# Two-layer hybrid trunk, one core: modulation on VectorE as product and sum, VectorE work given out by TensorE time

## The chip, the cores and the metric

The kernel runs on one core of a Trainium2 chip, with no other core at work. The metric is the device time of one execution in microseconds (us); a profiled execution gives a trace beside it. Five engines work in parallel, each in its own order: TensorE (PE; its weight loads are PEld), VectorE (DVE), ScalarE (ACT), GpSimd (POOL) and SyncE (SP), which here only issues DMAs.

## The reference, cut to what matters

```python
c_act = jax.nn.silu(c)                                   # (1, 2048)
for l in range(2):
    mod = c_act @ w_ada[l] + b_ada[l]                    # (1, 6*2048): the modulation
    sh1, sc1, gt1, sh2, sc2, gt2 = jnp.split(mod, 6, -1)
    h = rms_norm(x, g_norm1[l]) * (1 + sc1) + sh1        # x: 256 tokens x 2048
    # w_in -> q, k, v, indexer, u, p;  A: sparse attention -> o_a;
    # C: trailing means of p -> o_c;  B: diagonal complex state space of u:
    #   states = scan over time of lam_bar * state + b_bar @ u   (32 groups x 64 states)
    #   y = gelu((c_t @ states).real + d_skip * u);  o_b = y * sigmoid(y @ w_glu)
    mix = (sum of sigmoid(h @ w_gate[i] + b) * (o_i @ p_i) over the branches) @ w_out[l]
    x = x + gt1 * mix
    h = rms_norm(x, g_norm2[l]) * (1 + sc2) + sh2
    x = x + gt2 * conv_ffn(h, w_up, conv_w, conv_b, w_down)   # d_ff 5504
```

All weights are f32 and each is read once, so all of them pass through the chip's memory during the run.

## The kernel before

**The stream.** All weights but the modulation's are cut into 936 slots of 128x1024 f32 (512 KB; some 128x656). For each slot SP issues the load of `raw`, ACT rounds it to `whi` (fp32r, TensorE's fast f32 form), DVE makes `wlo = raw - whi`, and PE multiplies both halves with the activations. In most slots these are 8 matmuls `b<-h,whi` of 512 columns (high and low half of the activations side by side) and 8 `b<-h,wlo` of 256. `run_stream` (from L383) walks the slots: `make_hi(s+3)`, `make_lo(s+2)`, the slot's matmuls, then `step()`. The stages of a layer, in slots: q, k, v, u, p and the gates with the branch projections, `w_glu` at 160, `p_b`, the rest of the gates, `w_out` from 178, `w_up` from 210, `w_down` in two parts from 302 and 426; layer 1 begins at 468.

**Side work.** Everything else is written as Python generators, which `step()` advances. Their instructions are put down at that point of the program, so the order on every engine is fixed when the kernel is built. DVE tasks run while `credit` is above zero: a slot adds 2.6 us, each DVE operation takes off a price by its size (`tt`, `stt`, `ts`, L153 to L168), and the credit is kept between -2 and 2. `require` (L215) forces a task to its end where a slot needs its result: `yh` (the state-space output) before `w_glu`, `oc` (the pooling branch) before `p_c`, `ob` before `p_b`, `mod` before the norms.

**Modulation (`ada_group`, L504).** `w_ada` comes as 384 tiles `adaw` of 512 KB, through a ring of 4 (8 for the first 64). `ADA` lists the groups of tiles, `ADA_PLAN` how far they may be by which slot. 192 tiles are done on PE, in steps of two tiles (8 records `b<-adaw,cact`, four at a time in the four column groups); the other 192 on DVE, two operations a tile into `acc` (128x512, `acc<-adaw,cact,acc`), and after every 8 tiles four PE transposes (L573) and a `TENSOR_REDUCE` (L549) that sum `acc` over the partitions. The task is stepped ahead of the others; a group on PE is forced, one step at a time while its `yield 1` comes back, and so back to back.

**State space (`s5_tables`, `s5_task`).** Four blocks of channels are taken one after the other, in two pairs of state columns each; `prod` holds the rotated inputs, two scans a column run over time on DVE (L1090), and a pair's sine and cosine tables `tb` for the 256 times are built by doubling: ACT writes `pr`, DVE adds 16, 32, 64 and 128 columns at a time, so that DVE waits for ACT at each of four stages. `yp` sums `b<-prod,cc` on PE; `yt`, `u`, `yh` are the end of the chain.

Of the kernel before, what the change touches and what calls it, by code (L numbers as in the profile page):

```python
# [38 lines left out]
NRAW, NHI, NLO, NADA, APRE = 4, 4, 3, 4, 4  # L39
# [41 lines left out]
ADA_PLAN = ((0, 18), (8, 34), (18, 50), (30, 66), (48, 66), (140, 128), (204, 160), (296, 192), (460, 296), (580, 320), (670, 356), (770, 384))  # L81


ADA = [(0, [(1, t), (0, t)], 2 if t < 4 else 4, True) for t in (0, 2, 4, 8, 12)]
for _l in range(DEPTH):
    if _l:
        ADA += [(_l, [(p, t + j) for j in (0, 4) for p in (1, 0)], 4, False) for t in (0, 8)]
    ADA += [(_l, [(2, t) for t in range(0, 16, 4)], 4, not _l)]
    ADA += [(_l, [(p, t + j) for j in (0, 4) for p in (4, 3)], 4, not _l or t == 0) for t in (0, 8)]
    ADA += [(_l, [(5, t) for t in range(0, 16, 4)], 4, False)]  # L90

# [29 lines left out]
class Kernel:  # L121
    def __init__(self, ctx, tc, a):
# [19 lines left out]
        self.x_save = dpool.tile([128, KT, T], F32, name="x_save")  # L142
        ctx.enter_context(tc.manual_schedule())
# [9 lines left out]
    def tt(self, out, a, b, op):  # L153
        self.credit -= 0.069 + 1.04e-3 * self.size(out)
        self.nc.vector.tensor_tensor(out, a, b, op=op)  # L155

    def stt(self, out, a, s, b, op0, op1):
        self.credit -= (0.069 if isinstance(s, float) else 0.13) + 1.04e-3 * self.size(out)
        self.nc.vector.scalar_tensor_tensor(out, a, s, b, op0=op0, op1=op1)  # L159

    def ts(self, out, a, s1, s2, op0, op1=None):
        self.credit -= 0.069 + 0.7e-3 * self.size(out)
# [5 lines left out]
    def vcopy(self, out, a):  # L168
        self.credit -= 0.069 + 0.7e-3 * self.size(out)
        self.nc.vector.tensor_copy(out, a)  # L170
# [8 lines left out]
    def mm(self, out, lhsT, rhs, start=True, stop=True):  # L179
        self.nc.tensor.matmul(out, lhsT, rhs, start=start, stop=stop)  # L180
# [17 lines left out]
    def step_task(self, t, force=False):  # L198

        while force or (self.credit > 0 and self.acredit > -1.0):  # L200
# [7 lines left out]
    def step(self):  # L208
        self.step_evacs()
        for t in list(self.low):  # L210
            self.step_task(t, force=self.ada_on_pe)
        for t in list(self.tasks):
            self.step_task(t)

    def require(self, *keys):  # L215

        for key in keys:
            n = 0
            while key not in self.done:
                self.step_evacs()  # L220
                for t in self.tasks + self.low:
                    if key[0] in t[1] or n > 20:
                        self.step_task(t, force=True)
# [90 lines left out]
    def block_emitter(self, bl):  # L314
        def emit(hi, lo):
# [13 lines left out]
            for i, high in enumerate((True, False) if self.high_first else (False, True)):  # L329
                for u, j, x, cnt in todo:  # L330
                    out, w, r = (u.ps, hi, x) if high else (u.ps[:, T:], lo, x[:, :T])

                    self.nc.tensor.matmul(out, w[:, j * 128:(j + 1) * 128], r, start=i == 0 and cnt == 1,  # L333
                                          stop=i == 1 and cnt == u.nk, skip_group_check=True)
# [6 lines left out]
    def block(self, u, k, hi, lo):  # L341
# [16 lines left out]
        for i, (w, r) in enumerate(ops):  # L358
            self.nc.tensor.matmul(ps, w, r, start=first and i == 0 and not u.after,  # L359
                                  stop=last and i == 2 and not u.before, skip_group_check=shared)  # L360
# [22 lines left out]
    def run_stream(self):  # L383
        n = len(self.slots)
        for s in range(n):
# [7 lines left out]
            self.credit = max(min(self.credit + 2.6 * o.w / SLOT, 2.0), -2.0)  # L393
            self.acredit = max(min(self.acredit + 2.6 * o.w / SLOT, 2.0), -2.0)
# [100 lines left out]
    def ada_fetch(self, upto):  # L495
        while self.ada_next < upto:
            i = self.ada_next
            pool, bufs = self.ada_ring if i < 64 and i % (NADA + APRE) < APRE else (self.cpool, NADA)
            t = pool.tile([128, 1024], F32, name="adaw", tag="adaw", bufs=bufs)
# [1215 lines left out]
```

## Time and profile before

| | |
|---|---|
| median of 3 runs | 2950.82 us (2948.54 to 2952.45) |
| profiled execution | 2947.58 us, span 2945.8 us |
| PE busy | 2863.4 us, 97% of the span |
| DVE busy | 2301.6 us, 78% |
| ACT busy | 1395.1 us, 47% |
| DMA | 705.97 MB, mean 240 GB/s |

The span runs from the first instruction to the last of the profiled execution. Idle time of PE is 2945.8 - 2863.4 = 82.4 us. [...]

### The profile page before, as it was taken

What the parts mean: (1) busy time and instruction counts of PE and PEld (TensorE: products, weight loads), DVE (VectorE), ACT (ScalarE), POOL (GpSimd) and SP (SyncE); (2) the same over time, 40 slices, a digit from 0 to 9 for tenths busy, and PEclk for the clock granted to TensorE, in tenths of its full rate; (3) what the DMA queues carried; (4) which work ended last, traced back from release to release, by engine and by line L of the source; (5) the groups of instructions that cost most, each with busy time, mean ns of one, the idle gap of its engine ahead of it and who ended that gap; (6) DMA issues with size and microseconds to landing.
All of it is one profiled execution on the core that took longest, in us unless ns stands there. A gap on an engine that the chain in (4) does not pass through costs nothing.

```text
span 2945.8 us, 45105 instructions
## 1 busy us (share of the span) xinstructions
PE 2863.4 (97%) x16880; PEld 2427.5 (82%) x16880; DVE 2301.6 (78%) x4222; ACT 1395.1 (47%) x2209; POOL 43.7 (1%) x74
## 2 busy tenths in 40 slices
PE   6999999979999999999999999999999999999998
PEld 3787787758788888888878788888888888888887
DVE  5888677766698899999966887899888877556664
ACT  3355544434455543455435455455445555345542
POOL 0000000000000000000000000000000000000000
PEclk9999999979999999999999999999999999999999
DMA  9867767747677778888886555576686776566664
GB/s 366 349 225 254 238 243 253 248 145 279 209 263 251 251 270 296 297 287 298 299 315 205 194 180 182 192 245 241 230 283 211 241 237 204 192 189 188 189 198 150
DMA packets 195387, 705.97 MB, mean 240 GB/s; under 512 B 22496, under 2 KB 23008, under 8 KB 195168
## 3 DMA queue, kind: packets, MB, share of 16 engines
q1 hardware_dynamic: 190656, 691.23, 68.7%
q0 software_dynamic: 3648, 11.01, 1.0%
q8 instruction: 132, 2.16, 0.3%
q10 hardware_dynamic: 864, 0.86, 0.1%
q14 instruction: 87, 0.71, 0.1%
HBM read 698.82 MB, written 4.19 MB: 239 GB/s over the span
## 4 chain that ended last, share of the span: by engine, by line
PE 87%; issue 6%; DVE 4%; DMA 1%; ACT 0%; POOL 0%; POOLq 0%; SPq 0%; DVEq 0%; ACTq 0%
PE b L333 69%; PE b L180 11%; PE b L359 6%; DVE wlo L155 1%; DMA adaw<-in_w_ada 1%; DVE acc L159 0%; PE b L573 0%; DVE prod L155 0%; DVE x L159 0%; POOL out L1501 0%; PE b L917 0%; DVE prod L1090 0%; DVE ftmp L164 0%; DVE ftmp L155 0%; PE b L821 0%
## 5 line engine op out<-in xcount | busy, mean ns | idle before, releaser
L155 DVE TENSOR_TENSOR wlo<-raw,whi 128x1024 fp32r<-128x1024 f32 x936 | 1132.7, 1213 | 485.6 <-issue 220.1
L175 ACT ACTIVATE whi<-raw 128x1024 fp32r<-128x1024 f32 x936 | 984.1, 1053 | 1028.2 <-PE b L333 630.0
L333 PE MATMUL b<-h,whi 128*128 128x512 f32 x4352 | 1058.4, 393 | 4.3 <-DVE h L159 4.3
L333 PEld LDWEIGHTS b<-h,whi 128*128 128x128 f32 x4352 | 798.6, 189 | 168.9 <-issue 12.2
L333 PEld LDWEIGHTS b<-h,wlo 128*128 128x128 f32 x4352 | 562.5, 191 | 42.2 <-issue 11.3
L333 PE MATMUL b<-h,wlo 128*128 128x256 f32 x4352 | 578.5, 284 | 0.0
L333 PE MATMUL b<-hid,whi 128*128 128x512 f32 x1376 | 330.4, 391 | 2.6 <-DVE hid L159 2.6
L333 PEld LDWEIGHTS b<-hid,whi 128*128 128x128 f32 x1376 | 252.6, 188 | 52.1 <-DVE hid L159 3.4
L159 DVE SCALAR_TENSOR_TENSOR acc<-adaw,cact,acc 128x512 f32<-128x512 f32 x360 | 269.0, 747 | 5.6 <-DMA adaw<-in_w_ada 0.5
L333 PEld LDWEIGHTS b<-hid,wlo 128*128 128x128 f32 x1376 | 176.7, 191 | 9.5 <-DVE wlo L155 1.9
L333 PE MATMUL b<-hid,wlo 128*128 128x256 f32 x1376 | 180.0, 283 | 1.3 <-DVE wlo L155 1.3
L180 PE MATMUL b<-whi,h 128*128 128x512 f32 (+1 forms) x512 | 155.3, 376 | 0.0
L175 ACT ACTIVATE fth<-ft 128x256 f32<-128x256 f32 x86 | 36.0, 418 | 196.2 <-DVE ft L159 196.2
L333 PE MATMUL b<-mh,whi 128*128 128x512 f32 x512 | 123.6, 392 | 4.7 <-DVE mh L155 4.7
L180 PE MATMUL b<-adaw,cact 128*32 128x512 f32 (+1 forms) x832 | 111.2, 584 | 7.7 <-DMA adaw<-in_w_ada 7.7
L180 PEld LDWEIGHTS b<-whi,h 128*128 128x128 f32 x512 | 94.1, 188 | 27.9 <-issue 9.5
L333 PEld LDWEIGHTS b<-mh,whi 128*128 128x128 f32 x512 | 93.9, 188 | 23.9 <-DVE mh L155 3.7
L180 PE MATMUL b<-wlo,h 128*128 128x512 f32 (+1 forms) x256 | 94.9, 371 | 0.0
L359 PE MATMUL b<-h,whi 128*128 128x256 f32 x384 | 77.1, 297 | 10.4 <-ACT whi L175 5.4
L159 DVE SCALAR_TENSOR_TENSOR ft<-fa,lvecs,ft 128x255 f32<-128x255 f32 (+1 forms) x172 | 82.5, 481 | 3.1
L359 PEld LDWEIGHTS b<-h,whi 128*128 128x128 f32 x384 | 64.5, 202 | 15.6 <-ACT whi L175 6.5
L159 DVE SCALAR_TENSOR_TENSOR tb<-tb,nsn,pr 128x16 f32<-128x16 f32 (+3 forms) x128 | 35.4, 276 | 47.9 <-ACT pr L175 47.5
(262 smaller groups left out, 2539.0 us busy)
## 6 DMA issues: line engine op xcount, KB each, us to landing
adaw<-in_w_ada SPq DMA_DIRECT2D x384, 512.0 KB, 5.4
raw<-in_w_up SPq DMA_DIRECT2D x344, 512.0 KB, 3.9
raw<-in_w_gate SPq DMA_DIRECT2D x192, 512.0 KB, 3.9
raw<-in_w_down_a SPq DMA_DIRECT2D x88, 512.0 KB, 4.0
raw<-in_w_down_b SPq DMA_DIRECT2D x84, 512.0 KB, 4.4
raw<-in_w_out SPq DMA_DIRECT2D x64, 512.0 KB, 4.9
raw<-in_w_q SPq DMA_DIRECT2D x32, 512.0 KB, 3.9
raw<-in_p_a SPq DMA_DIRECT2D x32, 512.0 KB, 4.4
```

The source lines that it names most:

```text
L155: self.nc.vector.tensor_tensor(out, a, b, op=op)
L159: self.nc.vector.scalar_tensor_tensor(out, a, s, b, op0=op0, op1=op1)
L175: self.nc.scalar.activation(out, a, func, bias=bias, scale=scale)
L180: self.nc.tensor.matmul(out, lhsT, rhs, start=start, stop=stop)
L333: self.nc.tensor.matmul(out, w[:, j * 128:(j + 1) * 128], r, start=i == 0 and cnt == 1, stop=i == 1 and cnt == u.nk, skip_group_check=True)
L359: self.nc.tensor.matmul(ps, w, r, start=first and i == 0 and not u.after, stop=last and i == 2 and not u.before, skip_group_check=shared)
```

## The change

- **Modulation on DVE** becomes one `tensor_tensor_reduce` a tile: `adaw` (now laid out with output channels on partitions and 1024 inputs along the row) times `crow`, a row of the activated c replicated on all partitions, summed into one column of `mod`. On the engine each is two instructions, 128x1024 and a 128x1. No transposes and no `acc` are left there. `crow` is made at the start by 16 PE matmuls, 4 ACT copies and a 1 MB DMA to memory (`c_rows`), and loaded back half by half (512 KB, 8 times in all) by POOL's queue.
- **Credit** is earned by each PE instruction, by its columns (`earn`), not by slot; the prices of DVE operations rise by about 0.085 us each (the scan's from 0.68 to 1.35).
- **Order**: DVE's modulation is stepped after the other tasks, not before them; a PE step yields `None`, so one step (two tiles) comes per slot; `ADA` and `ADA_PLAN` are rearranged; the ring of 4 becomes a ring of 3 and a fourth tile shared with `crow` that serves until tile 160. `require` advances a forced task one yield at a time.
- **Tables**: the angles of 16 low and 16 high digits (`e0`, `e1`) are built once a layer; the tables of a pair are six DVE operations of 512 (products, sum and difference), without ACT.
- **`w_out`** begins with its first four output tiles interleaved by k, and the reload of x moves from its second to its sixth slot.

```diff
-NRAW, NHI, NLO, NADA, APRE = 4, 4, 3, 4, 4
+NRAW, NHI, NLO, NADA, APRE = 4, 4, 3, 3, 4
+ADA_FIRST, ADA_PE = 64, 160
     def tt(self, out, a, b, op):
-        self.credit -= 0.069 + 1.04e-3 * self.size(out)
+        self.credit -= 0.155 + 1.04e-3 * self.size(out)
...
+    def mm(self, out, lhsT, rhs, start=True, stop=True, share=1, **kw):
+        n = self.size(rhs)
+        self.earn((n + 32) / 2400 if rhs.dtype == F32R else n / 600 / share)
+        self.nc.tensor.matmul(out, lhsT, rhs, start=start, stop=stop, **kw)
...
     def step(self):
         self.step_evacs()
-        for t in list(self.low):
-            self.step_task(t, force=self.ada_on_pe)
+        low = list(self.low)
+        for t in low:
+            if self.ada_on_pe:
+                self.step_task(t, force=True)
         for t in list(self.tasks):
             self.step_task(t)
+        for t in low:
+            if t in self.low and not self.ada_on_pe:
+                self.step_task(t)
...
-            self.credit = max(min(self.credit + 2.6 * o.w / SLOT, 2.0), -2.0)
+            self.credit = max(min(self.credit, 2.0), -2.0)
...
-                yield 1
+            yield 1 if i < ADA_FIRST else None
...
+    def ada_sums(self, i0, l, tiles, first, ahead, last):
+        i = i0
+        for h in (first, 1 - first):
+            self.ada_on_pe = False
+            if self.crow_half != h:
+                self.crow = self.cpool.tile([128, 1024], F32, name="crow", tag="crow", bufs=1)
+                self.nc.gpsimd.dma_start(self.crow, self.c_rows[:, h * 1024:(h + 1) * 1024])
...
+            for part, t in tiles:
+                self.ada_fetch(min(i + ahead, last))
+                w = self.ada_tiles.pop(i)
...
+                self.credit -= 0.16 + 1.04e-3 * 1024
+                self.nc.vector.tensor_tensor_reduce(w, w, self.crow, 1.0, seed, OP.mult, OP.add, col)
...
+    def s5_tables(self, s):
+        tb = self.mx.tile([128, 2, 2, T], F32, name="tb", tag="tb")
+        pr = self.mx.tile([128, 2, T], F32, name="pr", tag="prod", bufs=2)
...
+            self.tt(out, hi[x[0]], lo[x[1]], OP.mult)
+            self.tt(p4, hi[y[0]], lo[y[1]], OP.mult)
+            yield 1
+            self.tt(out, out, p4, op)
...
-        self.slots[n + 1].pre = load_x
+        self.slots[n + 5].pre = load_x
...
-        o = [(n, k) for ks in (range(12), range(12, KT)) for n in range(4) for k in ks]
+        o = [(n, k) for k in range(KT) for n in range(4)]
```

Where instructions moved, first on DVE ahead of `w_glu` of layer 0. `prod` and `tb` are the state space, `yt` and `yh` its output that the next slot needs. Before, the last `wlo` ahead of `yh`, and the first rows behind it:

```order
L155 TENSOR_TENSOR wlo<-raw,whi 128x1024
L155 TENSOR_TENSOR prod<-prod 128x256 x2
L1090 SCALAR_TENSOR_TENSOR prod<-r,prod 128x256 x2
L159 SCALAR_TENSOR_TENSOR prod<-prod,tb 128x256
L155 TENSOR_TENSOR prod<-prod,tb 128x256
L155 TENSOR_TENSOR prod<-prod,tb 128x2x256
```

Between the last of these and `yh` stand 33 more rows: the 16 `tb` rows of a pair's tables, one of the gates, two chains with scans and the four rows of `yt` and `u`. After, from the last `wlo` ahead of `yh` to the next:

```order
L163 TENSOR_TENSOR wlo<-raw,whi 128x1024
L167 SCALAR_TENSOR_TENSOR prod<-prod,tb 128x256
L163 TENSOR_TENSOR prod<-prod,tb 128x256
L163 TENSOR_TENSOR prod<-prod,tb 128x2x256
L163 TENSOR_TENSOR th_5985<-th_5985,b_6092 128x256
L167 SCALAR_TENSOR_TENSOR yt<-u,lvecs,b_5659 128x256
L174 TENSOR_SCALAR yt<-yt 128x256
L163 TENSOR_TENSOR yt<-yt 128x256
L167 SCALAR_TENSOR_TENSOR u<-yt 128x256
L163 TENSOR_TENSOR yh<-u,yh 128x256 x4
L163 TENSOR_TENSOR wlo<-raw,whi 128x1024 x2
```

The tables of the last pair and two chains with scans went to earlier slots; the last three `prod` rows and the chain of `yt` are what is still behind that `wlo`.

Second, on PE, the end of the first layer's `w_down`, where five steps of modulation stood in a row before:

```order
L573 MATMUL b_15201<-const,acc 128x128 x4
L333 MATMUL b_15156<-hid,whi 128x512 x6
L333 MATMUL b_15212<-hid,whi 128x512 x2
L333 MATMUL b_15156<-hid,wlo 128x256 x6
L333 MATMUL b_15212<-hid,wlo 128x256 x2
L180 MATMUL b_15232<-adaw,cact 32x512 x20
L333 MATMUL b_15212<-hid,wlo 128x256 x8
L333 MATMUL b_15212<-hid,whi 128x512 x16
```

Those 20 are gone from the end of `w_down`; that part of the modulation is on DVE now. The group that PE does in layer 1 now stands around the beginning of `p_c` (`oc` matmuls), one step in a slot, in seven slots that follow one another; its first steps:

```order
L191 MATMUL b_17452<-adaw,cact 32x512 x4
L191 MATMUL b_17469<-h,whi 128x512 x8
L191 MATMUL b_17469<-h,wlo 128x256 x8
L191 MATMUL b_17452<-adaw,cact 32x512 x4
L191 MATMUL b_17498<-kT,qT 128x256 x2
L191 MATMUL b_17469<-h,wlo 128x256 x8
L191 MATMUL b_17469<-h,whi 128x512 x8
L191 MATMUL b_17452<-adaw,cact 32x512 x4
L191 MATMUL b_17544<-p,wp 128x256 x2
```

Each step stands alone behind a slot's 16 matmuls, with a ring of three tiles behind it. (The trace has two records for each of these matmuls: a step is x4 here and x8 there.)

Third, on DVE, the pooling branch ahead of `p_c` in layer 0. `lg` and `mxv` belong to the attention, `oa` to its output. Before:

```order
L155 TENSOR_TENSOR wlo<-raw,whi 128x1024 x2
L155 TENSOR_TENSOR th<-th,b_3795 128x256
L159 SCALAR_TENSOR_TENSOR oc<-b_3849,lvecs,oc 128x256 x2
L159 SCALAR_TENSOR_TENSOR oc<-b_3852,lvecs,oc 128x256 x2
L155 TENSOR_TENSOR wlo<-raw,whi 128x1024
```

There `oc` has a stretch of its own, behind one row of the gates. After:

```order
L163 TENSOR_TENSOR wlo<-raw,whi 128x1024
L163 TENSOR_TENSOR lg<-b_3956,isc 128x512
L962 TENSOR_REDUCE mxv<-lg 128x2
L172 TENSOR_SCALAR mxv<-mxv 128x2
L968 RECIPROCAL mxv<-mxv 128x2
L172 TENSOR_SCALAR lg<-lg,mxv 128x256 x2
L163 TENSOR_TENSOR th<-th,b_3908 128x256
L167 SCALAR_TENSOR_TENSOR oc<-b_3974,lvecs,oc 128x256 x2
L167 SCALAR_TENSOR_TENSOR oc<-b_3984,lvecs,oc 128x256 x2
L163 TENSOR_TENSOR prod<-b_3901,tb 128x512 x2
L163 TENSOR_TENSOR prod<-prod 128x256 x2
```

`oc` now comes behind a piece of attention in the same stretch between two `wlo`.

## Rows read from the trace of the kernel before

**Rows 1.** The page's first part: busy us, share of the span, instructions.

```profile
PE 2863.4 (97%) x16880; PEld 2427.5 (82%) x16880; DVE 2301.6 (78%) x4222; ACT 1395.1 (47%) x2209; POOL 43.7 (1%) x74
```

**Rows 2.** Waits of PE: waited-for work, us in total, times, longest us.

```profile
PE b L180 <- DVE prod L155: 14.7, 4, 6.6
...
PE b L180 <- DMA adaw<-in_w_ada: 7.7, 12, 2.0
...
PE b L359 <- ACT yh L175: 5.1, 2, 2.6
PE b L333 <- DVE mh L155: 4.7, 2, 3.1
```

**Rows 3.** Windows: stretch, its us, busy us by engine, PE's clock, DMA share, GB/s.

```profile
606.00:634.00 28.00, 11.27 (x42) 4.39 (x42) 19.16 (x50) 6.95 (x19) 0.00 (x0) 0.55 0.10 35
213.00:606.00 393.00, 393.00 (x2397) 309.82 (x2396) 301.80 (x641) 191.36 (x358) 6.35 (x9) 1.00 0.71 243
1050.00:1500.00 450.00, 446.86 (x2581) 394.19 (x2581) 431.40 (x749) 208.03 (x278) 5.96 (x11) 1.00 0.84 295
...
54.00:64.00 10.00, 7.38 (x32) 1.00 (x28) 2.56 (x15) 0.60 (x3) 0.00 (x0) 1.00 1.03 417
...
633.60:639.20 5.60, 5.57 (x24) 5.33 (x24) 1.54 (x6) 0.90 (x3) 0.00 (x0) 0.50 0.01 3
```

**Rows 4.** Timeline of DVE ahead of `w_glu`, layer 0: start us, us, instructions, count.

```profile
606.00 1.21 DVE L155 TENSOR_TENSOR wlo<-raw,whi 128x1024 fp32r<-128x1024 f32 x1
...
633.64 0.76 DVE L155 TENSOR_TENSOR yh<-u,yh 128x256 fp32r<-128x256 f32 x2
```

**Rows 5.** Timeline of PE there; in brackets its idle us before and the releaser.

```profile
610.64 3.62 PE L180 MATMUL b<-prod,cc 128*32 128x256 f32 x14 [4.06 <-DVE prod L155]
...
622.88 1.06 PE L180 MATMUL b<-prod,cc 128*32 128x256 f32 x2 [6.61 <-DVE prod L155]
627.45 3.62 PE L180 MATMUL b<-prod,cc 128*32 128x256 f32 x14 [3.50 <-DVE prod L155]
633.63 0.58 PE L359 MATMUL b<-yh,whi 128*128 128x256 f32 x1 [2.56 <-ACT yh L175]
```

**Rows 6.** Timeline of PE at the same place of layer 1.

```profile
2056.79 1.91 PE L180 MATMUL b<-prod,cc 128*32 128x256 f32 x14 [0.49 <-DVE prod L155]
2061.27 0.39 PE L359 MATMUL b<-yh,whi 128*128 128x256 f32 x1 [2.56 <-ACT yh L175]
```

**Rows 7.** Timeline of PE at the end of layer 0's `w_down`: the modulation's five steps.

```profile
1517.06 1.91 PE L180 MATMUL b<-adaw,cact 128*32 128x512 f32 x12
1519.93 1.05 PE L180 MATMUL b<-adaw,cact 128*32 128x512 f32 x4 [0.97 <-DMA adaw<-in_w_ada]
...
1531.75 1.22 PE L333 MATMUL b<-hid,wlo 128*128 128x256 f32 x8
```

**Rows 8.** Timeline of PE: four transposes between two matmuls of the stream.

```profile
1513.72 0.60 PE L573 MATMUL b<-const,acc 128*128 128x128 f32 x4
1514.08 2.10 PE L333 MATMUL b<-hid,whi 128*128 128x512 f32 x8
```

**Rows 9.** Groups of DVE by line and form: count | busy us, mean ns | idle before.

```profile
L155 DVE TENSOR_TENSOR wlo<-raw,whi 128x1024 fp32r<-128x1024 f32 x920 | 1119.6, 1220 | 475.6 <-issue 214.7 <-PE b L333 175.3 <-PE b L180 29.0
L159 DVE SCALAR_TENSOR_TENSOR acc<-adaw,cact,acc 128x512 f32<-128x512 f32 x360 | 269.0, 747 | 5.6 <-DMA adaw<-in_w_ada 0.5
...
L1090 DVE TENSOR_TENSOR_SCAN prod<-r,prod 128x256 f32<-128x256 f32 x64 | 40.4, 672 | 0.0
...
L159 DVE SCALAR_TENSOR_TENSOR hid<-ft,hid 128x256 fp32r<-128x256 f32 x86 | 35.8, 419 | 1.4 <-ACT hid L175 1.4
...
L549 DVE TENSOR_REDUCE mod<-b 128x4 f32<-128x512 f32 x24 | 16.4, 682 | 0.0
...
L155 DVE TENSOR_TENSOR lg<-b,isc 128x512 f32<-128x512 f32 x12 | 8.2, 687 | 3.9 <-PE b L180 3.9
```

**Rows 10.** DMA issues: queue, count, KB each, median us from issue to landing.

```profile
adaw<-in_w_ada SPq DMA_DIRECT2D x384, 512.0 KB, 5.4
raw<-in_w_up SPq DMA_DIRECT2D x344, 512.0 KB, 3.9
```

More of the change, by code (lines that the diff above doesn't have):

```diff
@@ L142, in __init__ @@
         self.x_save = dpool.tile([128, KT, T], F32, name="x_save")
+        self.c_rows = dpool.tile([128, 2048], F32, name="c_rows")
         ctx.enter_context(tc.manual_schedule())
@@ L168, in vcopy @@
     def vcopy(self, out, a):
-        self.credit -= 0.069 + 0.7e-3 * self.size(out)
+        self.credit -= 0.15 + 0.6e-3 * self.size(out)
         self.nc.vector.tensor_copy(out, a)
@@ L219, in require @@
             while key not in self.done:
[L220 to L223, printed above, removed]
+                mine = [t for t in self.tasks + self.low if key[0] in t[1] or n > 60]
+                if n % 3 == 0 or not mine:
+                    self.step_evacs()
+                for t in mine:
+                    self.step_task(t, once=True)
+                    if key in self.done:
+                        break
                 n += 1
@@ L358, in block @@
         for i, (w, r) in enumerate(ops):
-            self.nc.tensor.matmul(ps, w, r, start=first and i == 0 and not u.after,
-                                  stop=last and i == 2 and not u.before, skip_group_check=shared)
+            self.mm(ps, w, r, start=first and i == 0 and not u.after, stop=last and i == 2 and not u.before,
+                    skip_group_check=shared)
         if last:
@@ new lines, in ada_group @@
+    def ada_group(self, i0, l, chunks, wt, ahead, last):
+        m = len(chunks)
+        self.ada_on_pe = True
+        b, ps = yield from self.take_bank()
+        i, n, width = i0, wt // 2, 128 * wt
+        for q in range(0, KT, 4 // m):
+            self.ada_fetch(min(i + n, last))
+            ws = [self.ada_tiles.pop(i + j) for j in range(n)]
+            for g in range(4):
+                k = q + g // m
+                cs = self.cact[:, k:k + 1].to_broadcast([128, 32])
+                w = ws[g * n // 4][:, g * width % 1024:][:, :width]
+                self.mm(ps[32 * g:32 * g + 32, :width], cs, w, start=q == 0, stop=q + 4 // m == KT, share=4)
+            i += n
+            self.ada_fetch(min(i + ahead, last))
+            while self.ada_early(i):
+                yield None
+            yield 1 if i < ADA_FIRST else None
@@ L584, in ada_task @@
         i = sum(2 * wt * len(chunks) for _, chunks, wt, _ in ADA[:lo])
-        for l, chunks, wt, on_pe in ADA[lo:hi]:
-            yield from self.ada_group(i, l, chunks, wt, on_pe, ahead, last)
+        for l, chunks, wt, first in ADA[lo:hi]:
+            if first is None:
+                yield from self.ada_group(i, l, chunks, wt, ahead, last)
+            else:
+                yield from self.ada_sums(i, l, chunks, first, ahead, last)
             i += 2 * wt * len(chunks)
```

237 lines of the change are left out of this document (118 added, 119 removed).

## The prediction

> **What bounds the kernel now.** I read the busy times first: PE is busy 2863.4 us of 2945.8 [rows 1], so at most 82.4 us can be won by filling its gaps; more only by giving PE less work or a faster clock. Then the windows: from 213 to 606 us PE has no gap at all at clock 1.00 while DVE is busy 301.8 of 393, 77% [rows 3]; from 1050 to 1500, in the first layer's FFN, PE is busy 446.86 of 450 and DVE 431.40, 96% [rows 3]. So DVE's load as such costs PE nearly nothing, but in the FFN it has only 4% to spare: what the change adds per slot there is the first thing to price. Third, PE's waits, read for the places where side work is forced on it. Waits for `prod` are 14.7 us in 4 pieces, for `adaw` 7.7 in 12, for `yh` 5.1 in 2, for `mh` 4.7 in 2 [rows 2]. Last, the timelines at these places, since a gap is followed there by a lower clock, which no list of waits shows.
>
> **1. The end of the state space before `w_glu`, layer 0.** Behind the last `wlo` DVE still does the tables of a pair and two chains with scans, from 606.00 until `yh` at 633.64 [rows 4]. [...] The first `yh` matmuls run 5.57 us at 0.50, 2.8 us more than at full clock [rows 3]. After the change one `wlo` (1.22 us [rows 9]), three `prod` operations, one operation of the gates and the chain of `yt` stand there. Layer 1 of before has just such an end and shows its price: from 2056.79 to 2061.27, 4.48 us, of which 2.56 idle behind the `prod` matmuls [rows 6]. To that I add three `prod` operations and a `th` of about 0.42, 0.42, 0.69 and 0.42 us (by the sizes of rows 9) and the `wlo`: 3.2 us. [...] Gain 27.6 - 7.7 - 3 = 17 us. I leave the slow `yh` matmuls as they are, since layer 1 ran slowly there after a much shorter gap. Between 12 (half clock stays for longer) and 20.
>
> **2. The same place in layer 1.** `yt` and `yh` are made about seven slots earlier in the new order. The idle 0.49 + 2.56 [rows 6] goes, and the matmuls behind it no longer follow a gap: I add 2 us for the clock, less than the 2.8 of layer 0. Gain 5 us, between 3 and 6.
>
> **3. The burst at the end of `w_down`, layer 0.** Five steps run from 1517.06 to 1531.75, 14.7 us [rows 7], forced back to back and so paced by the loads. A step that doesn't wait takes 1.05 us [rows 7], so 5.3 are work (192 tiles stay on PE, the work goes elsewhere) and 9.4 are lost. Gain 9.4, with one answer.
>
> **4. The transposes.** 24 groups of `acc`, as the TENSOR_REDUCE is counted [rows 9], each cost PE 1514.08 - 1513.72 = 0.36 us [rows 8]; 24 x 0.36 = 8.6 us of PE time that goes for good. Gain 8.5.
>
> **5. `w_out` by k.** The first slot needs two `mh` tiles and not twelve. Gain up to the 4.7 us of [rows 2]; I take it whole. The later reload of x has three slots' time less; I cost it at nothing, covered by eight slots before the first output tile ends.
>
> Gains together: 17 + 5 + 9.4 + 8.5 + 4.7 = 44.6 us, with 37 and 49 as ends.
>
> **6. The new operation on DVE.** No row shows a product with a sum. From below: `wlo` has the same size and two sources from SBUF and takes 1.22 us; the read-out of the sum is another small instruction, for which I take the fixed part of an operation. By `hid` and `lg` that is 0.419 - 256 x (0.687 - 0.419) / 256 = 0.15 us [rows 9]; together 1.37. From above: the scan takes 0.672 us for 256 elements, so (0.672 - 0.15) / 256 = 2.04 ns for one; 1024 of them and two fixed parts are 2.39. A tile cost 2 x 0.747 + 0.682 / 8 = 1.58 before [rows 9]. I take 1.4, near `wlo`, since the sum doesn't hand a value from one output element to the next as a scan does. Then DVE has less to do in the FFN, and as PE has only 3 us of gaps in that window anyway, it gains nothing: 0.
>
> [...]
>
> **7. PE's group in layer 1.** Seven steps stand in slots that follow one another, with a ring of three tiles. A step uses two; the third is there for the next step, but its second tile is loaded only after a release. A load takes 5.4 us to land at the median [rows 10], and a slot's 16 matmuls cover 446.86 / 2581 x 16 = 2.8 us of it [rows 3]. That leaves 2.6 us of wait a step, or 1.1 if they land as fast as `raw`, 3.9 us [rows 10]; seven steps cost 8 to 18 us, and I take 2 each: 14. From below 5, if matmuls of `p_c` and attention cover more of it; from above 30, if the clock falls to half for the 20 us behind such waits, as at 633.6 [rows 3].
>
> **8. `oc` ahead of `p_c`.** It now stands behind attention work in the same stretch: a `lg` of 0.69, a reduction of 0.68, four small ones, one `th` and four `oc` operations of about 0.42 [rows 9], some 4.5 us with what ACT does between. DVE runs ahead of PE there (77% busy), which covers part: 2.5 us, the middle of 0 and 4.5; in layer 1 a similar place, 3. Cost 5.5.
>
> **9. Start and rest.** The copy `c_rows` of 1 MB comes while DMAs move 417 GB/s at a full share [rows 3]: 1.05 MB / 417 GB/s = 2.5 us. The 16 matmuls and four copies that make it lie in gaps of the start. The later 512 KB reloads have a queue of their own and four steps of lead: 0. Four products in a row at one place of layer 1, waiting for their tiles: 2. DVE now waits for PE where ACT did before (`prod` ring): 2, from 0 to 5.
>
> Costs together: 14 + 5.5 + 2.5 + 2 + 2 = 26 us, with 8 and 45 as ends.
>
> **Sum.** 2947.6 us (the profiled execution, span and what lies around it) - 44.6 + 26 = 2929 us. The profile lies 3.2 us below the median of the runs shown, 2950.82; I predict against that median, but halfway to it: 2931.
>
> **The rivals.**
> (a) *The product and sum runs at two cycles an element* (2.39 us). In the FFN of layer 0 the order has 0.66 of these tiles in a slot over 148 slots. DVE's load there is 0.96 x 2.8 = 2.68 us a slot; 0.66 x (2.39 - 1.58) = 0.53 more makes 3.21 against PE's 2.8: 148 x 0.42 = 62 us lost. 2931 + 62 = 2993, slower than before. It decides from a price of 1.58 + (2.8 - 2.68) / 0.66 = 1.76 us. For it: the scan's row, and no row of a sum at all. [...]
> (b) *The new waits eat the gain*: the ring of three with its clock (30), `oc` at its full 9, the gap of layer 0 only halved (12): 2948 - 39.6 + 45 = 2953, no change. For it: wherever PE waited for several us in a row the clock was seen at 0.5 to 0.55 [rows 3].
> (c) *The new waits are covered* and costs are 8 or less: about 2907. For it: the loads land in 3.9 us where the memory isn't full, and DVE has room.
> (d) *The tail isn't shortened*, because DVE is late at the earlier slots and PE waits there instead: 2931 + 17 = 2948. Against it: 91 us of DVE's time are free between 213 and 606 [rows 3], and the moved work is under 28.
>
> **How the numbers follow.** My forecast, 2915 to 2944, has 0.58; (c) 0.16; (b) and (d) together 0.14; (a) 0.09; another slowdown 0.03. The range 2904 to 2958 takes in all but (a) and the tails. A measurement tells 0.2% from no change, 5.9 us. Faster than 2945: 0.76; within: 0.11; slower: 0.13.
>
> **What would show it.** Each step has a row in the profile after. The wait for `yh` and `prod` before `w_glu` should be under 7 us in sum, in layer 1 none; 1510 to 1535 should be full; the waits of PE for `adaw` should have moved to layer 1's `p_c` and be near 14 us; the transposes of line L573's kind should count 32 records and not 128. The first number to read is the mean of the product with sum: at 1.4 us the sum stands, above 1.76 it is wrong, and DVE's share in the FFN would say so. The prediction is also wrong if PE's clock in the new gaps stays at half for longer than the gaps.

## The result, and the profile after

The changed kernel takes 2928.31 us at the median (2924.98 to 2929.63, 4 runs) against 2950.43 us of the kernel before: a ratio of 0.9926, 95% interval 0.9914 to 0.9938. The prediction was 2931. The profiled execution took 2929.02 us with a span of 2927.2, 18.6 us less than the span before; the prediction's sum went from 2947.6 to 2929. So the total came out nearly exactly, but not the way it was put together: the rows below show two costs that were forecast and for the most part did not come, and others of the same size that came unforeseen.

The page's first part, after (as [rows 1]), and the waits of PE with their us, times and longest us (as [rows 2]; lines have other numbers after the change, L191 for matmuls, L163 to L174 for VectorE):

```profile
PE 2856.5 (98%) x16816; PEld 2422.8 (83%) x16816; DVE 2271.7 (78%) x4064; ACT 1353.1 (46%) x2053; POOL 49.8 (2%) x83
```

```profile
PE b L689 <- DVE sqa L163: 6.5, 3, 3.3
PE b L191 <- DVE wlo L163: 6.2, 6, 3.2
PE b L689 <- ACT sq L183: 6.0, 3, 3.0
PE b L191 <- ACT pt L183: 5.0, 2, 3.6
...
PE b L191 <- DMA adaw<-in_w_ada: 4.2, 10, 1.1
PE b L191 <- ACT yh L183: 3.0, 1, 3.0
```

The waits for `prod` and `mh` are gone, those for `yh` went from 5.1 to 3.0. Those for `wlo` went from 2.0 to 6.2 and those for the squares `sq` of the norm from 4.2 to 6.0. Their running sum `sqa` was waited for once before, at the start; now it is waited for 5.3 us at the two norms of layer 0. Waits for `pt`, the attention's weights, are new. Before:

```profile
PE b L629 <- DVE sqa L155: 14.2, 1, 14.2
...
PE b L629 <- ACT sq L175: 4.2, 3, 1.8
...
PE b L333 <- DVE wlo L155: 1.3, 2, 0.7
PE b L359 <- DVE wlo L155: 0.7, 1, 0.7
```

I summed the bracketed gaps of PE's timeline by stage, and beside them what a low clock cost: in windows of 10 us, busy time times one less the granted clock (the trace shows it as a share of the full one, which is 1.00). The slow matmuls right behind the wait for `yh` count to the stage up to `w_glu`.

| stage | idle before, after | lost to the clock before, after |
|---|---|---|
| start, to 66 us | 27.6, 23.9 | 4.1, 6.1 |
| layer 0 up to `w_glu` | 17.5, 3.9 | 8.5, 1.4 |
| `p_b`, gates, `w_out`, norm | 6.7, 7.8 | 2.6, 4.7 |
| FFN of layer 0, norm | 11.4, 14.0 | 2.7, 6.0 |
| layer 1 up to `w_glu` | 3.1, 7.4 | 1.5, 4.5 |
| `p_b`, gates, `w_out`, norm | 7.6, 4.5 | 2.3, 2.2 |
| FFN of layer 1 | 0.7, 0.7 | 0, 0 |
| all | 74.6, 62.1 | 21.6, 25.0 |

One stage, the first layer up to `w_glu`, gave 20.7 us, more than the whole gain. The FFN of layer 0, its norm and layer 1's attention gave back 13 of it. Idle time and clock together make 9 us of the 18.6. The rest is PE work that fell away: there are 32 transposes of `acc` where there were 128.

The place ahead of `w_glu`, layer 0: a window (stretch, its us, busy us by engine, clock, DMA share, GB/s) and two rows of PE's timeline (start us, us, count, idle before and releaser), to be read against [rows 3, 5]:

```profile
598.00:620.00 22.00, 19.02 (x113) 13.97 (x112) 16.38 (x30) 9.75 (x18) 0.00 (x0) 0.95 0.64 226
```

```profile
611.21 2.52 PE L191 MATMUL b<-prod,cc 128*32 128x256 f32 x16
616.70 0.39 PE L191 MATMUL b<-yh,whi 128*128 128x256 f32 x1 [2.96 <-ACT yh L183]
```

One gap of 2.96 us stands where four of 16.73 us in all stood, and the clock is 0.95, not 0.55.

The new operation, by line and form (count | busy us, mean ns | idle before, and its releaser), as [rows 9]:

```profile
L602 DVE CUSTOM_DVE_ANT_0 adaw<-adaw,crow,vecs 128x1024 f32<-128x1024 f32 x96 | 122.5, 1279 | 27.0 <-DMA adaw<-in_w_ada 26.9
L602 DVE CUSTOM_DVE_ANT_0 adaw<-adaw,crow,mod 128x1024 f32<-128x1024 f32 x96 | 122.2, 1279 | 10.1 <-DMA adaw<-in_w_ada 9.9
...
L602 DVE DVE_READ_ACCUMULATOR2_ANT mod<- 128x1 f32 x192 | 15.7, 82 | 0.0
```

A tile costs 1.279 + 0.082 = 1.36 us. What the prediction priced for one place alone, at 2 us, stands in the last column: VectorE waits 36.9 us in 17 pieces for the tiles. Such a wait holds up all that is behind it in VectorE's order. In `w_down` of layer 0 and at the norm behind it, VectorE first and then PE:

```profile
1441.59 1.28 DVE L602 CUSTOM_DVE_ANT_0 adaw<-adaw,crow,vecs 128x1024 f32<-128x1024 f32 x1
...
1446.99 1.28 DVE L602 CUSTOM_DVE_ANT_0 adaw<-adaw,crow,vecs 128x1024 f32<-128x1024 f32 x1 [4.11 <-DMA adaw<-in_w_ada]
...
1448.20 1.22 DVE L163 TENSOR_TENSOR wlo<-raw,whi 128x1024 fp32r<-128x1024 f32 x1
...
1512.01 1.28 DVE L602 CUSTOM_DVE_ANT_0 adaw<-adaw,crow,mod 128x1024 f32<-128x1024 f32 x1 [1.04 <-DMA adaw<-in_w_ada]
...
1514.36 0.42 DVE L163 TENSOR_TENSOR sqa<-sqa,sq 128x256 f32<-128x256 f32 x1
1514.70 1.27 DVE L602 CUSTOM_DVE_ANT_0 adaw<-adaw,crow,mod 128x1024 f32<-128x1024 f32 x1
...
1517.04 1.00 DVE L167 SCALAR_TENSOR_TENSOR x<-b,mod,x 128x256 f32<-128x256 f32 x2
```

```profile
1449.47 1.21 PE L191 MATMUL b<-hid,wlo 128*128 128x256 f32 x8 [3.15 <-DVE wlo L163]
...
1514.92 0.58 PE L689 MATMUL b<-const,sqa 128*128 128x1 f32 x4 [3.27 <-DVE sqa L163]
1518.54 1.01 PE L689 MATMUL b<-const,sq 128*128 128x1 f32 x4 [3.04 <-ACT sq L183]
```

Two products in one step, the second without its tile: `wlo` is 4.11 us late, and PE waits 3.15. At the norm one product, whose tile is 1.04 us late, stands ahead of the last `sqa`, and a second one ahead of the last `x`, from which ScalarE makes `sq`. PE waits 3.27 and 3.04 us there; before it waited only for `sq`, 1.21 us. Behind that the clock is low:

```profile
1505.00:1525.00 20.00, 11.12 (x56) 9.49 (x55) 14.66 (x28) 6.72 (x11) 2.34 (x4) 0.76 0.80 287
```

### The profile page after: what moved, and what is told of

Its sections match the earlier page's. It is cut to its first block, busy times and chain, and to the rows that moved or that the text cites. A ratio compares the mean times of both kernels' runs of the same rounds, so it can differ in the third digit from the quotient of the medians.

```text
span 2927.2 us, 44510 instructions
## 1 busy us (share of the span) xinstructions
PE 2856.5 (98%) x16816; PEld 2422.8 (83%) x16816; DVE 2271.7 (78%) x4064; ACT 1353.1 (46%) x2053; POOL 49.8 (2%) x83
## 4 chain that ended last, share of the span: by engine, by line
PE 91%; issue 3%; DMA 3%; DVE 2%; ACT 1%; POOL 0%; ACTq 0%; POOLq 0%; SPq 0%; DVEq 0%
PE b L191 90%; DMA adaw<-in_w_ada 2%; DVE wlo L163 1%; PE b L195 0%; DMA raw<-in_w_kv 0%; DVE adaw L602 0%; DMA posi<-in_pos 0%; POOL out L1557 0%; DVE x L167 0%; ACT whi L183 0%; DVE sqa L163 0%; ACT lg L185 0%; POOL rv L699 0%; ACT h L183 0%; DVE nt L167 0%
## 5 line engine op out<-in xcount | busy, mean ns | idle before, releaser
L163 DVE TENSOR_TENSOR wlo<-raw,whi 128x1024 fp32r<-128x1024 f32 x936 | 1133.0, 1214 | 480.2 <-issue 252.5
L191 PE MATMUL b<-h,whi 128*128 128x512 f32 (+1 forms) x4736 | 1133.8, 385 | 15.4 <-DVE h L167 9.1
L191 PEld LDWEIGHTS b<-h,whi 128*128 128x128 f32 x4736 | 866.4, 191 | 187.7 <-issue 18.6
L191 PE MATMUL b<-h,wlo 128*128 128x256 f32 x4544 | 634.4, 285 | 1.1 <-DVE wlo L163 1.1
L191 PEld LDWEIGHTS b<-h,wlo 128*128 128x128 f32 x4544 | 602.8, 192 | 38.9 <-issue 9.4
L191 PE MATMUL b<-hid,whi 128*128 128x512 f32 x1376 | 331.0, 392 | 1.6 <-DVE hid L167 1.6
L191 PEld LDWEIGHTS b<-hid,whi 128*128 128x128 f32 x1376 | 254.0, 189 | 51.7 <-DVE hid L167 2.4
L191 PEld LDWEIGHTS b<-hid,wlo 128*128 128x128 f32 x1376 | 176.6, 191 | 11.7 <-DVE wlo L163 5.1
L191 PE MATMUL b<-hid,wlo 128*128 128x256 f32 x1376 | 179.5, 283 | 4.3 <-DVE wlo L163 4.3
L191 PE MATMUL b<-whi,h 128*128 128x512 f32 (+1 forms) x512 | 154.4, 375 | 0.0
L602 DVE CUSTOM_DVE_ANT_0 adaw<-adaw,crow,vecs 128x1024 f32<-128x1024 f32 x96 | 122.5, 1279 | 27.0 <-DMA adaw<-in_w_ada 26.9
L602 DVE CUSTOM_DVE_ANT_0 adaw<-adaw,crow,mod 128x1024 f32<-128x1024 f32 x96 | 122.2, 1279 | 10.1 <-DMA adaw<-in_w_ada 9.9
L191 PE MATMUL b<-mh,whi 128*128 128x512 f32 x512 | 123.2, 391 | 0.0
L191 PEld LDWEIGHTS b<-whi,h 128*128 128x128 f32 x512 | 94.0, 188 | 26.6 <-issue 9.8
L191 PE MATMUL b<-adaw,cact 128*32 128x512 f32 (+1 forms) x832 | 109.1, 579 | 4.4 <-DMA adaw<-in_w_ada 4.2
L191 PEld LDWEIGHTS b<-mh,whi 128*128 128x128 f32 x512 | 93.8, 188 | 20.5 <-issue 2.5
L191 PE MATMUL b<-wlo,h 128*128 128x512 f32 (+1 forms) x256 | 94.9, 371 | 0.0
L191 PEld LDWEIGHTS b<-mh,wlo 128*128 128x128 f32 x512 | 65.8, 191 | 6.2 <-issue 1.7
L167 DVE SCALAR_TENSOR_TENSOR x<-b,mod,x 128x256 f32<-128x256 f32 x128 | 61.4, 481 | 9.3 <-PE b L191 7.0
```

The costliest lines, as they stand in the source:

```text
L602: self.nc.vector.tensor_tensor_reduce(w, w, self.crow, 1.0, seed, OP.mult, OP.add, col)
```

## The experiments

The theory after reading both traces: the credit, not the cheaper tables, moves the state space ahead of `w_glu`; transposes, the burst and `w_out` give what their rows say; and the price of the ring of three is paid on VectorE, by products that wait for tiles ahead of `wlo` and of the norm. Differences in us below are to the 2928.31 of the changed kernel where nothing else is said; ratios are to the kernel before, with 95% intervals.

**What moves the state space: credit or tables.** The first run gives credit by slot again and takes the prices of before (from its edit):

```diff
-        self.earn((n + 32) / 2400 if rhs.dtype == F32R else n / 600 / share)
...
-            self.credit = max(min(self.credit, 2.0), -2.0)
+            self.credit = max(min(self.credit + 2.6 * o.w / SLOT, 2.0), -2.0)
```

> The changed kernel with the credit and the prices of before: 2.6 us for a slot whatever else TensorE does in it, 0.069 + 1.04 ns an element for a VectorE operation; everything else as changed. Theory (the credit moves the state space ahead of w_glu): some of the second pair's work (4 table rows, 2 scans) stands again between the last wlo and yh, so PE waits 8 to 12 us there at half clock and the time is 2938 to 2946. Rival (cheap tables and the order of the modulation task carry the gain, the credit is only bookkeeping): within 4 us of the changed kernel, 2925 to 2932.

2935.08 us, 0.9951 (0.9936 to 0.9966): 7 us slower, between the two expectations. Its waits show why:

```profile
PE b L190 <- DVE wlo L163: 15.9, 12, 4.0
PE b L190 <- DVE prod L163: 12.3, 3, 6.9
```

The wait for `prod` ahead of `w_glu` is back, and the curve of its matmuls (the start of the n-th matmul of the stream, against the changed kernel's) is 17.5 us behind there. In the FFN of layer 0 it falls to 32 us behind, by waits for `wlo`: there VectorE has many small operations of layer 1's tables in front of `wlo`, which the old prices put too low (0.086 us for 128x16, where such operations take 0.17 to 0.19 in the trace of the changed kernel). Later it regains some: it has no wait for `sqa` at the second norm and none for `pt`, and ends 13 us behind in the profiled execution, the slowest of its four. So the theory holds for the place. Credit and prices were changed together, here and in the third run; which of them does it was not told apart. The second run takes the tables of before with the new credit:

```diff
-        tb = self.mx.tile([128, 2, 2, T], F32, name="tb", tag="tb")
+        tbs = [self.mx.tile([128, 2, T], F32, name="tb", tag="tb", bufs=2) for _ in pair]
...
+                self.act(prs[:, i, :, :n], tb[:, 0:2, :n], AF.Copy, scale=p5.cs[:, j:j + 1])
```

> The changed kernel with the tables of before (doubling, 16 small VectorE operations and 10 on ScalarE a pair). Theory (credit carries the gain): the rows between the last wlo and yh stay the 8 of the changed kernel, PE does not wait longer for yh, and the time is within 0.2% of the changed one, 2924 to 2934. Rival (the tables carry the gain, since VectorE waited 47.5 us for ScalarE's pr in them): PE waits for prod by 10 us or more, 2938 to 2946.

2927.0 us, 0.992 (0.9905 to 0.9935): no difference, as the theory had it. VectorE waits 52.4 us for `pr` again, but PE waits 2.96 us for `yh` as in the changed kernel. The tables carry nothing of the gain as long as the credit is the new one.

The third puts the new credit and prices into the kernel before:

```diff
-    def mm(self, out, lhsT, rhs, start=True, stop=True):
-        self.nc.tensor.matmul(out, lhsT, rhs, start=start, stop=stop)
+    def mm(self, out, lhsT, rhs, start=True, stop=True, share=1, **kw):
...
+        self.earn((n + 32) / 2400 if rhs.dtype == F32R else n / 600 / share)
...
-            self.credit = max(min(self.credit + 2.6 * o.w / SLOT, 2.0), -2.0)
+            self.credit = max(min(self.credit, 2.0), -2.0)
```

> The kernel before with one thing of the change: credit by the time of all TensorE work, and the new prices. The modulation is still stepped first. Theory (the credit moves the state space only together with the new order of tasks, for the modulation takes the higher credit first): layer 0 has less work ahead of w_glu, 14 rows and one scan, which gives 8 to 12 us; layer 1 now has 65 rows there with four scans, which costs 20 to 30 us, and eight PE steps stand in a row; 2955 to 2980 in all. Rival (the credit alone carries the gain): 2930 to 2940.

2980.26 us, 1.0099 (1.0084 to 1.0114): 30 us slower than the kernel before, at the upper end of the theory. Layer 0 reaches `yh` some 4 us earlier than before, but layer 1 has the whole end of the state space in front of `w_glu`:

```profile
PE b L183 <- DVE prod L155: 29.6, 7, 10.3
```

Credit alone is not the gain. That the modulation is stepped first was my reason; the next run speaks against it:

```diff
         for t in low:
-            if self.ada_on_pe:
-                self.step_task(t, force=True)
+            self.step_task(t, force=self.ada_on_pe)
         for t in list(self.tasks):
             self.step_task(t)
-        for t in low:
-            if t in self.low and not self.ada_on_pe:
-                self.step_task(t)
```

> The changed kernel with VectorE's modulation stepped ahead of the other tasks again. By the order of instructions as little stands ahead of yh as in the changed kernel. Theory (the plan, not the place in the step, sets how many products stand in a stage): within 0.2% of the changed kernel, 2923 to 2934. Rival (products then stand ahead of attention and evacuations that PE waits for): PE's waits for pt, lg, wlo and sqa (18 us with the start) grow by 5 us or more, 2934 to 2945.

2923.28 us, 0.991 (0.9895 to 0.9925): 5 us faster than the changed kernel, at the edge of the theory's range and not clear of noise (some 5.7 us either way). PE waits 2.96 us for `yh` again, so the place in the step is not what keeps the state space early. The waits for `pt` and `lg` in layer 1 are gone, those for `wlo` are 11.0 us. PE's single steps are not the credit's partner in layer 1 either: the next run takes them back and has no wait for `prod` or `yh`. Left are the plan, the cheaper operations of the modulation and the forced tasks that advance by one yield; which of them it is was not told apart.

**The burst.** In the changed kernel, PE's steps back to back again:

```diff
-            yield 1 if i < ADA_FIRST else None
+            yield 1
```

> The changed kernel with PE's modulation steps forced back to back again, as before the change; in layer 1 seven steps (28 rows) then stand in a row. Theory (a burst is paced by its loads): seven steps of 1.06 us of work take 7 x 2 x 1.25 us = 17.5 us at the rate of the loads at the start, so 10 us are lost there, 2934 to 2942. Rival (the loads are ahead by then and the ring of three covers it as it covered single steps, 0.7 us of wait): within 0.2%, 2923 to 2934.

2942.16 us, 0.9971 (0.9961 to 0.9981): 14 us slower, just beyond the upper end of the theory. The waits of PE for tiles went from 4.2 to 14.6 us:

```profile
PE b L191 <- DMA adaw<-in_w_ada: 14.6, 21, 2.5
```

The opposite edit in the kernel before, `yield 1 if i < 64 else None`:

> The kernel before with one thing of the change: one PE step of the modulation a slot after the first 64 tiles, not forced back to back. Theory (the burst at the end of w_down costs 9.4 us, as 14.7 us for 5.3 us of work): 2938 to 2944. Rival (the steps wait singly for their loads, or PE waits at the norm behind them): 2946 to 2954.

2942.79 us against 2950.28, 0.9974 (0.9963 to 0.9984): 7.5 us, inside the theory's range. The burst of layer 0 is worth 7.5 us by itself where it was priced at 9.4.

**The transposes** (24 groups of four, of a constant, added to the changed kernel):

```diff
+                if i % 8 == 0:
+                    b, ps = yield from self.take_bank()
+                    for j in range(4):
+                        self.nc.tensor.transpose(ps[:, j * 128:(j + 1) * 128], self.ident, self.ident)
...
```

> The changed kernel with four PE transposes of a constant added after every 8 products, 24 groups as before the change; nobody reads them. Theory (each group costs PE 0.355 us): 8.5 us more, 2934 to 2940. Rival (they fall into gaps that PE has anyway): within 0.2%, 2924 to 2932.

2933.72 us, 0.995 (0.9934 to 0.9967): 5.4 us slower, just below the theory's 2934. In the FFN of layer 0, where nothing else moved, its curve falls back by 4.3 us between 802 and 1324 us; 10 of the 24 groups stand there, so one costs 0.43 us. By that, 24 would cost some 10 us (an estimate); other gaps (`pt`) happened to close, which hides a part of it in the total.

**`w_out` by k**, undone in the changed kernel, with the reload of x:

```diff
-        o = [(n, k) for k in range(KT) for n in range(4)]
+        o = [(n, k) for ks in (range(12), range(12, KT)) for n in range(4) for k in ks]
```

> The changed kernel with the order of w_out and the place of the reload of x as before. Theory (the first slot waits for twelve mh tiles): PE waits for mh again, 4 to 5 us in two places, and the time is 2931 to 2936. Rival (the mh tiles are made earlier now, as the state space no longer holds them up): 2925 to 2931, no wait for mh over 1 us.

2936.87 us, 0.9955 (0.994 to 0.997): 8.6 us slower (some 5.7 either way), a little beyond the theory. Two waits for `mh` are back, but they are shorter than expected:

```profile
PE b L191 <- DVE mh L163: 3.2, 2, 2.4
```

By the curve of the matmuls, 4.2 us are lost around layer 0's `w_out` and its norm and 4.9 us around layer 1's. In layer 0 these are 1.4 us of idle for `mh`, 1.6 more for `wlo` ahead of the norm, and a rest that no wait shows; the clock stays at 1.00 behind the `mh` wait. In layer 1 they are 2.35 us of idle and 1.7 of slow clock behind it.

**What the new operation may cost.** Each product twice:

```diff
+                junk = self.cpool.tile([128, 1], F32, name="junk", tag="junk", bufs=1)
                 self.nc.vector.tensor_tensor_reduce(w, w, self.crow, 1.0, seed, OP.mult, OP.add, col)
+                self.nc.vector.tensor_tensor_reduce(w, w, self.crow, 1.0, seed, OP.mult, OP.add, junk)
```

> The changed kernel with each product-and-sum done twice (the second sum goes to a column that nobody reads), and no credit taken for the second. A tile then costs VectorE 2 x 1.36 = 2.72 us, near the 2.39 us of rival (a). Theory (VectorE sets the time of the FFN once a tile costs over some 1.8 us): VectorE was busy 397 of 447 us there, 2.49 us of a slot's 2.8; with 0.66 tiles a slot it needs 2.49 + 0.66 x 1.36 = 3.39, so 148 slots lose 0.59 each, 87 us, and the time is 2995 to 3035, PE waiting for wlo. Counter-theory (PE's stream absorbs it, since wlo is made two slots ahead): under 2950.

3064.58 us, 1.0386 (1.0365 to 1.0406): 136 us slower, by the theory's mechanism and beyond its range.

```profile
PE b L191 <- DVE wlo L163: 82.3, 66, 4.4
```

```profile
1030.00:1570.00 540.00, 484.35 (x2610) 417.81 (x2610) 519.09 (x913) 214.14 (x296) 7.01 (x13) 0.96 0.74 244
```

VectorE is at 96% there and PE at 90. PE's idle time grew by 88 us, 76 of it for `wlo` (82 us against 6), most of the rest at the norms and for `hid`. The slow clock lost 50.3 us over the span where it lost 25.0, which the expectation had left out. Some 20 us of the 136 I cannot assign. So rival (a) of the prediction was a real way to lose and hung on one price alone; its own 2.39 us was not run.

**Products and their loads.** One product a step (`yield None` for `yield 1` in `ada_sums`):

> The changed kernel with at most one product-and-sum in a step. Theory (the price of the ring of three falls on VectorE: it waits 36.9 us in 17 pieces for adaw when two products come in one step, and wlo and sqa behind it come late): VectorE's wait for adaw falls below 15 us, PE's waits for wlo and sqa (6.2 and 6.5 us) below 3 and 4, and the time falls by 5 to 12 us, to 2916 to 2923. Rival (the products themselves stand in front of wlo and sqa, not their loads): the waits of PE stay, time within 0.2%.

2928.22 us, 0.9925 (0.9908 to 0.9942): the same time, as the rival had it, though the waits went the theory's way. VectorE's wait for tiles fell from 36.9 to 12.9 us, PE's for `wlo` and `sqa` from 6.2 and 6.5 to 1.8 and 3.4:

```profile
PE b L191 <- DMA adaw<-in_w_ada: 7.2, 15, 1.3
...
PE b L689 <- DVE sqa L163: 3.4, 3, 2.0
...
PE b L191 <- DVE wlo L163: 1.8, 2, 1.1
```

The profiled execution, the fastest of the four, was 6.4 us shorter than that of the changed kernel; the median shows none of it. In its trace PE waits for tiles in layer 1 instead, where its group now stands later. This run alone settles nothing. The next two add a plan with no products ahead of the norms (pieces of `ADA_PLAN`, as slot and tile):

```diff
-(200, 162), (240, 165), (300, 196), (462, 288),
+(196, 162), (214, 162), (300, 196), (452, 288), (474, 288),
```

> The changed kernel with at most one product in a step and a plan that puts no product into the last ten or so slots before the two norms of layer 0. Theory (VectorE comes late to the norms because products and their loads stand ahead of the last squares): PE's waits for sqa fall from 6.5 us to about 1.2, the clock at 770 to 790 and 1510 to 1530 stays higher, and the time is 2916 to 2923. Rival (the waits at the norm come from the chain of the last output tile itself): sqa unchanged, 2924 to 2932.

2925.98 us, 0.9917 (0.9902 to 0.9932): the first norm is as wished (no wait for `sqa`), the second still waits 1.64 and 3.04 us, for products that come late against the plan. The last run gives them room, by more products in `w_up` (against the run just shown):

```diff
-(196, 162), (214, 162), (300, 196), (452, 288), (474, 288),
+(196, 162), (214, 162), (300, 202), (444, 288), (474, 288),
```

> The changed kernel with one product a step and another plan: more products during w_up, none from slot 444 to 474 unless they are late. Theory (what is left of the wait for sqa at the second norm is products that come late against the plan): sqa and wlo below 2.5 us together, 2917 to 2924. Rival (the norm's chain and a clock that falls behind any gap set the rest): 2924 to 2930.

2915.99 us (2914.18 to 2916.89), 0.9884 (0.9869 to 0.9899): 12 us faster than the changed kernel, 10 us (some 6 either way) faster than the run just before by the plan alone, and the fastest of all here. Its waits of PE:

```profile
PE b L689 <- ACT sq L183: 4.2, 3, 1.8
...
PE b L689 <- DVE sqa L163: 2.9, 2, 1.6
...
PE b L191 <- ACT pt L183: 2.1, 1, 2.1
PE b L191 <- DVE wlo L163: 1.9, 3, 1.0
```

`sqa` and `wlo` are 4.8 us together, not under 2.5 as I wanted, but PE idles 54.6 us where it did 62.1 and loses 19.2 to the clock where it lost 25.0. Against the changed kernel it is 12.1 us ahead when layer 1's first block is under way, 13.5 at the end: what it wins, it wins at the two norms and in `w_down`, where the theory had put the loss. All runs of the changed kernel keep the ring of three, so what the ring's length costs by itself was not measured.

## Why the prediction was right, step by step

**Step 1, the end of the state space in layer 0.** Right in kind, a little short. Predicted gain 17; idle and slow clock of that stage fell by 20.7, after the 0.9 us that `oc` costs in it. From the last `wlo` to the first `yh` matmul it now takes 7.55 us (609.15 to 616.70), where the sum has 7.7. No run shows the 3 us that the sum takes off for matmuls which leave the stretch: by busy time times clock PE's work in it was 11.27 x 0.55 = 6.2 us before and is 4.57 us at 1.00 now, 1.6 less. What I added to layer 1's pattern, a `wlo` and three `prod` operations, hardly showed as idle time: PE still had matmuls to do while VectorE made them, and only the 2.96 us for `yh` were left.

**Step 2, layer 1.** Right: both gaps, 3.05 us, and 1.5 of slow clock are gone; predicted 5.

**Step 3, the burst.** 9.4 predicted, 7.5 by the run that takes it out of the kernel before. But the sentence on the profile after, that 1510 to 1535 should be full, was wrong. In place of the burst on PE there are products on VectorE, and with their late tiles that stage lost more than the burst had cost. (In the rows of this group `x4` is half a step, one of its two tiles; a whole step, `x8`, also takes 1.06 us [the rows under step 7], so the 1.05 that the prediction took for a step was the right number.)

**Step 4, the transposes.** Right as far as it can be told: 0.36 us a group predicted, 0.43 measured where nothing else moved. The whole run lost 5.4 us with an interval of about 6 either way, against 8.5.

**Step 5, `w_out`.** 4.7 predicted, and both waits for `mh` are gone. Undone in the changed kernel it costs 8.6, of which only 3.7 are waits for `mh`; 1.7 are a slow clock behind one of them. In the kernel before, from which the term was read, the clock was 1.00 behind both (from 693.4 to 699 and from 2119.05 to 2129 us), so the term was right there, and what the order is worth depends on the kernel around it.

**Step 6, the new operation.** Right: 1.4 predicted, 1.36 measured, and no loss from its price in the FFN. The rows of 1279 ns with the sum and of 1220 for `wlo` without one, both over 1024 elements, differ by 0.059 us; the read-out of the sum is an instruction of its own, in the row of 82 ns. The traces give VectorE's times in ns and no cycle of it, so what can be read of rival (a)'s two cycles is its 2.39 us. Less the prediction's 0.15 us of fixed part, the rows come to 1.10 ns an element for the product with its sum, 1.04 for `wlo` and 2.04 for the scan (estimates from 1.279, 1.220 and 0.672 us).

**Step 7, PE's group in layer 1, was the wrong term.** Predicted 14 us, measured some 3.5. Its first seven steps after:

```profile
1775.21 2.10 PE L191 MATMUL b<-adaw,cact 128*32 128x512 f32 x8
...
1780.23 1.05 PE L191 MATMUL b<-adaw,cact 128*32 128x512 f32 x4
1781.97 1.05 PE L191 MATMUL b<-adaw,cact 128*32 128x512 f32 x4 [0.69 <-DMA adaw<-in_w_ada]
...
1786.81 1.06 PE L191 MATMUL b<-adaw,cact 128*32 128x512 f32 x8
...
1802.61 1.82 PE L191 MATMUL b<-adaw,cact 128*32 128x512 f32 x8
```

Between the last two stand two more of 1.06 us, behind them one. Three of the seven lose time: the second tile comes late (TensorE's weight loads wait 0.90, 1.60 and 0.62 us for it), and the two halves of the step run one after the other, which takes 2.10, 2.79 (with 0.69 of idle) and 1.82 us instead of 1.06. The tiles issued from 1700 to 1800 us:

```profile
DMA to landing us min/median/max: 3.3/4.9/6.2
```

The step that failed is the cover of the load: from one step to the next it takes 4.1 to 6.8 us, not the 2.8 of 16 matmuls on which the term rested, since the slots there also carry attention, pooling and the change's own step of 1.06 us. The loads land in 4.9 us at the median and are mostly covered. The waits for tiles stand on the other engine instead: VectorE takes two products in a step with no work between them and waits 36.9 us. That the shorter ring makes these waits is argued, not shown; one product a step takes them to 12.9 us with the same ring.

**Step 8, `oc`.** 5.5 predicted, 0.9 measured (0.21 and 0.71 us ahead of `p_c`, layer 0; none in layer 1). VectorE had run far enough ahead.

**Step 9, the start and the rest.** 2.5 predicted for the start; by 100 us the two kernels were level to 0.2 us. The 2 us for products in a row are the one place where this kind of loss was foreseen, and it was put down far too small. Three places lost. They are the end of `w_down` with its norm (idle and clock 5.9 us more, beside the burst's own gain), the norm behind `w_out` (3.2 more in its stage, though the wait for `mh` went) and the attention of layer 1, where `pt` comes 3.63 and 1.40 us late and the clock cost 4.5 us. The 1.40 us stand behind four products in a row, one of which waits 3.74 us for its tile. The 3.63 us do not: in front of them VectorE has no product for over 100 us. There ScalarE has `pt` behind the exponentials of the next piece of attention, and these wait for VectorE's `mxv`; the clock is low behind the gap for 9 us (rows of ScalarE, and a window as in [rows 3]):

```profile
1694.00 0.40 ACT L185 ACTIVATE lg<-lg,mxv 128x128 f32<-128x128 f32 x1 [4.87 <-DVE mxv L172]
...
1697.16 0.57 ACT L183 ACTIVATE pt<-b 128x512 f32<-128x512 f32 x1
```

```profile
1697.79:1706.94 9.15, 9.15 (x27) 6.05 (x28) 7.11 (x13) 1.49 (x2) 0.54 (x1) 0.51 0.62 202
```

That is a term of the new order that no step of the prediction has, and it is the sign that the prediction named last against itself: half clock for longer than the gap.

So of the costs of 26 us some 20 did not come (10.5 of step 7, 4.6 of `oc`, 4.5 of the start and the `prod` ring), and others of about that size did; the gains were right to a few us each. The total was right by the gains, which were understood, and by two errors in the costs that happened to cancel; the second is luck. Rival (b), new waits that eat the gain, was the nearest in kind to what happened from the first norm on, though not at the places that it named; the run with the better plan won 12 us of it back. The reason given for (b), that the clock was at 0.5 to 0.55 wherever PE waited for several us in a row, does not hold in the trace of before: behind the 3.10 us for `mh` the clock is 1.00 from 2119.05 to 2129.

## What to carry to other kernels

A wait priced for one engine can be paid by another: look at every engine that draws on a ring of tiles, and first at the one that takes two in a row with nothing between. To price the cover of a load, take the distance between the two uses in the new order with everything that stands there, not the main stream's work alone. Work put off to the end of a stage collides with the chain that closes it (here the norm); a plan that is quiet there, with one product a step, was worth 12 us here, where taking the finer credit back cost 7.

## What the runs showed of the hardware

A product of two f32 rows with a sum over 1024 elements took 1.279 us and its read-out 0.082, against 1.220 us for the plain difference `wlo` of the same size in the kernel before; a scan took 0.672 us for 256 elements. A matmul over 256 columns took 0.283 us with both operands in fp32r (`h` and `wlo`) and 0.379 in f32 (`pt` and `v`), medians of the kernel before from 213 to 606 us at clock 1.00.

In the changed kernel a single gap of PE was followed by matmuls at half clock. From 600 to 611 us PE was busy all the time at clock 1.00. Behind the 2.96 us ahead of `w_glu` the clock was 0.84 from 616.70 to 618.43 and 0.50 from there to 621.0, where the pair of `yh` matmuls that takes 0.40 us at 1.00 took 0.63:

```profile
618.43 0.63 PE L191 MATMUL b<-yh,whi 128*128 128x256 f32 x2
...
621.49 0.40 PE L191 MATMUL b<-yh,whi 128*128 128x256 f32 x2
```

But the length of the gap alone does not tell. Nearly the same gap at the same matmul, the first of `w_down` in layer 0, was followed by a low clock in the last run of the experiments and by none in the one with the tables of before (a row of the timeline and the 6 us behind it, the last run first):

```profile
1398.06 0.50 PE L191 MATMUL b<-hid,whi 128*128 128x512 f32 x1 [1.95 <-DVE hid L167]
1398.06:1404.06 6.00, 6.00 (x27) 5.37 (x28) 4.48 (x7) 1.66 (x3) 0.55 (x1) 0.72 0.52 175
...
1402.47 0.50 PE L191 MATMUL b<-hid,whi 128*128 128x512 f32 x1 [1.94 <-DVE hid L167]
1402.47:1408.47 6.00, 6.00 (x34) 5.31 (x35) 4.43 (x8) 2.63 (x4) 0.55 (x1) 1.00 0.46 180
```

So the clock behind a short gap cost between 0 and some 1.7 us here, and a price for it that is read off one trace can be off by that much at each gap. The slow clock cost the kernel with each product twice 50 us in all, where most of its gaps were 66 single ones for `wlo` of up to 4.4 us.
